# A hybrid attention / state-space / mixture-of-experts layer: queries and keys computed with channels on partitions instead of tokens

## The chip, the cores and the metric

The kernel runs on one core of one Trainium2 chip. The metric is the device time of one execution in microseconds (us).

## The reference, cut to what matters

The layer normalises 1024 latent tokens and 256 context tokens, multiplies them by one wide weight `w_in`, runs differential attention beside a bidirectional state-space scan, merges both, and then applies a mixture of experts. The change touches the part that makes queries and keys. Each of the 8 heads has two halves of 64 channels; latent tokens get a rotary embedding that pairs channel i with channel i + 32 of the half, context keys get none.

```
q, k, v, z, xbc, dt_raw, gates = jnp.split(h @ w_in, IN_SPLITS, axis=-1)
q = apply_rope(q.reshape(nb, ns, N_ATTN_HEADS, 2, ATTN_DH), cos, sin)
k = apply_rope(k.reshape(nb, ns, N_ATTN_HEADS, 2, ATTN_DH), cos, sin)
kc = (hc @ w_k).reshape(nb, nl, N_ATTN_HEADS, 2, ATTN_DH)
k_all = jnp.concatenate([kc, k], axis=1)
s = jnp.einsum('bqhcd,bkhcd->bchqk', q, k_all) * ATTN_SCALE
```

```
def apply_rope(u, cos, sin):
    rot = jnp.concatenate([-u[..., 32:], u[..., :32]], axis=-1)
    return u * cos[:, None, None, :] + rot * sin[:, None, None, :]
```

## The kernel before, in words

Products in float32 accuracy are made of three matmuls on split operands: high by high, low by high and high by low (`mm3`; hi, lo are the two parts of the weights, hh, hl those of the normalised tokens). The order of all instructions is set when the kernel is built, by a planner (the class of `F`): every job is a generator that says what it needs next, and the planner advances the job that its own cost clocks find ready first. The engines then run their parts of that order one instruction after the other.

`norm_and_qkv` is the first stage. It computes six blocks of 512 columns of `w_in`, in the order k0, v0, q0, k1, v1, q1; a block holds four heads. `weights()` loads a block in two halves (`raw`) and splits them, the cast to `hi` on ACT and the subtraction to `lo` on DVE. `main()` in `norm_and_qkv` then takes the tiles of 128 tokens one after the other (two of context and eight latent ones for k and v, eight for q). For every tile the tokens are the stationary operand (128x128) and the 512 weight columns move: 24 matmuls into one of four PSUM banks (`acc`). So tokens stand on partitions in the result. Scores need channels on partitions, so `post_qk` does this for each tile of q or k: three rope operations on DVE (`ra`, and `rb` twice), an addition on POOL (`r`), four transposes on PE (`tr<-cst,r`), a cast of the transposed tile on ACT (`sa`) and the subtraction of the low part on DVE (`sb`). After every second tile SP issues the stores of `sa` and `sb` to the DRAM tensors `qk[0]` and `qk[1]`. These hold [128, 3328] for a half of a head in one piece: 64 channels by high and by low part, and in a row the queries twice and the keys.

Beside that, `ada_late` runs chains of multiply-adds on DVE (`wacc<-wada,cc,wacc`, chunks of eight instructions) and small matmuls on PE (`adab`). Before the first tiles PE also transposes the tokens (`tr<-cst,x`), and DVE and ACT normalise and split them.

The next stage begins with the dt job, whose matmuls `acc<-hh,hi 64x512` are the first after q1: it ends in a chain that goes from PE (`aux<-fold`) over DVE, ACT (absolute value, exponential, logarithm) and DVE back to PE (`aux<-dtn`). The matmuls of the convolution's inputs (`acc<-hh,hi 128x512`) follow.

Much later `attention_ahead` loads a half of a head at a time into a ring of three SBUF tiles `qk` ([128, 3328], 1664 KB). POOL issues these loads (`F.swdma`, line 1338); a load is issued when PE has finished with the tile whose place it takes. PE's scores `sps<-qk` wait for it.

The rotary table `rope` is loaded once, as [128, 8, 128] (512 KB).

Of the kernel before, what the change touches and what calls it, by code (L numbers as in the profile page):

```python
# [9 lines left out]
F32 = mybir.dt.float32  # L10
# [39 lines left out]
def host_consts():  # L50
    j = np.arange(P)
    eye = np.eye(P, dtype=np.float32)
    le = (j[:, None] <= j[None, :]).astype(np.float32)
    ge = (j[:, None] >= j[None, :]).astype(np.float32)
    ones = np.ones((P, P), np.float32)
    cst = np.concatenate([eye, le, ge, ones], axis=1)
    row = np.repeat(np.arange(T // 64, dtype=np.float32), 64)
    col = np.tile(np.arange(64, dtype=np.float32), T // 64)
    inv = np.float32(10000.0) ** (-np.arange(0, 32, 2, dtype=np.float32) / np.float32(32))
    inv = inv.astype(np.float32)  # L60
    ang = np.concatenate([row[:, None] * inv, col[:, None] * inv], axis=-1)
    cos, sin = np.cos(ang), np.sin(ang)
    rope = np.concatenate([cos, cos, -sin, sin], axis=-1).astype(np.float32)
    e = np.arange(64)
    iota = np.zeros((P, 260 + sum(LEVELS)), np.float32)
    iota[:, 0:64] = e
    iota[:64, 64:128] = e[None, :] < e[:, None]
    iota[:, 128:192] = np.tile((e[:8, None] > e[None, :8]).reshape(-1), 1)
    iota[:, 192], iota[:, 193], iota[:, 194] = j, j // 64, j // 32
    iota[:, 196:260] = CAPS  # L70
    slots = [j % (P // ways(min(P, c - P * lv))) + P * lv for lv, nr in enumerate(LEVELS) for c in CAPS[:nr]]
    iota[:, 260:] = np.stack(slots, axis=1)
    return {"cst": cst, "rope": rope, "iota": iota}
# [303 lines left out]
class Layer:  # L377
# [114 lines left out]
    def norm_and_qkv(s):  # L492
# [25 lines left out]
        cw = ap.tile([P, KC, 32], F32, name="cw")  # L518
        F.dma(craw[:, 0, :], I["c"].rearrange("b (p k) -> p (b k)", p=P))
        F.dma(craw[:, 1, :], I["c_ctx"].rearrange("(p k) -> p k", p=P))  # L520
        st = {"wa": [], "x": 0, "w": 0, "normed": 0, "mod": 0, "done": [set(), set(), set()], "cols": 0, "blocks": 0, "ada": False, "q": None, "two": {}}
        AX0, AW0, QS, NH = (2, 2, 4, 4, 6, 6, 8, 8, 8, 8), (2, 6), (0, 2, 1, 3), 3
        blocks = [("k", 0), ("v", 0), ("q", 0), ("k", 1), ("v", 1), ("q", 1)]
        ready = []
# [103 lines left out]
        def parts(g, k, hf, w):  # L628
# [5 lines left out]
            hfs.put(hf)  # L634
            st["done"][g].add(k)

        def weights():
            for n, (kind, j) in enumerate(blocks):
                c0 = {"q": COL_Q, "k": COL_K, "v": COL_V}[kind] + j * 512
                for a in (0, 4):  # L640
                    yield [raws, lambda: st["x"] >= (10 if n else AW0[a // 4]), "NOW"]
                    raw = raws.get()
                    F.dma(raw, win[:, a:a + 4, c0:c0 + 512])
                    st["w"] += 1
                    yield [lambda: sets[n % 2] is not None]
                    his, los = sets[n % 2]
                    yield [raw, his, los, "ACT"]
                    hi, lo = his.get(), los.get()
                    yield from s.splits([(hi[:, b:b + 2], lo[:, b:b + 2], raw[:, b:b + 2]) for b in (0, 2)],
                                        lambda raw=raw, w=(hi, lo): (raws.put(raw), ready.append(w)), 1)  # L650

        def post_v(ps, j, tok):
# [6 lines left out]
            F.dma(s.vv[j][tok], v[:, :512].rearrange("p (h d) -> p h d", d=P))  # L659
            sas.put(v)  # L660

        def post_qk(ps, kind, j, t):
            yield [lambda: st["q"] is not None]
            rr, ras, rbs, sas, sbs, rope = (st["q"][n] for n in ("r", "ra", "rb", "sa", "sb", "rope"))
            if t < 2:
                yield [ps, rr, "ACT"]
                r = rr.get()
                F.acopy(r, ps.rearrange("p (h x) -> p h x", x=64))
                acc.put(ps)
            else:  # L670
                yield [ps, rope, ras, rbs, "DVE"]
                cs = rope[:, t - 2, :]
                pv = ps.rearrange("p (h x) -> p h x", x=64)
                ra, rb = ras.get(), rbs.get()
                F.tt(ra, pv, cs[:, None, 0:64].to_broadcast([P, 8, 64]), ALU.mult)
                F.tt(rb[:, :, 0:32], pv[:, :, 32:64], cs[:, None, 64:96].to_broadcast([P, 8, 32]), ALU.mult)
                F.tt(rb[:, :, 32:64], pv[:, :, 0:32], cs[:, None, 96:128].to_broadcast([P, 8, 32]), ALU.mult)
                acc.put(ps)
                yield [ra, rb, rr, "POOL"]
                r = rr.get()  # L680
                F.ptt(r, ra, rb, ALU.add)
                ras.put(ra)
                rbs.put(rb)
            yield [r, tr]
            pt = tr.get()
            for m in range(4):
                F.tp(pt[:, m * P:(m + 1) * P], r[:, 2 * m:2 * m + 2].rearrange("p u x -> p (u x)"), s.ident)
            two = st["two"].setdefault((kind, j, t // 2), [])
            yield [pt, "ACT"] + ([] if two else [sas, sbs])
            if not two:  # L690
                two += [sas.get(), sbs.get(), 0]
            a, b = two[:2]
            (av, bv), pv = (w.rearrange("p (m h c) -> h p m c", m=4, h=2)[t % 2] for w in (a, b)), pt.rearrange("p (m c) -> p m c", m=4)
            F.acopy(av, pv)
            yield [a, "DVE"]
            F.tt(bv, pv, av.bitcast(F32), ALU.subtract)
            tr.put(pt)
            two[2] += 1
            if two[2] == 2:
                o0 = (t // 2 - (kind == "q")) * 2 * P  # L700
                dst = s.qk[j].rearrange("(m u) (v x) c -> v u x m c", u=2, v=2)
                for w, v, o in ((a, 0, 0), (a, 1, 0), (b, 0, T), (b, 1, T)) if kind == "q" else ((a, 0, 2 * T), (b, 1, 2 * T)):
                    for u in range(2):
                        F.dma(dst[v, u][:, :, o + o0:o + o0 + 2 * P], w[64 * u:64 * u + 64].bitcast(F32).rearrange("x (m c) -> x m c", m=4))
                sas.put(a)
                sbs.put(b)
            rr.put(r)

        def main():
            for n, (kind, j) in enumerate(blocks):  # L710
                tiles = list(range(2 if kind == "q" else 0, 10))
                steps = [(t, 0, KC) for t in tiles]
                if n == 0:
                    steps = [(t, a, a + 4) for a in (0, 4) for t in tiles[:NH]] + steps[NH:]
                banks = {}
                for t, k0, k1 in steps:
                    yield [lambda: len(ready) >= 2 * n + k1 // 4]
                    tok = slice(t * P, (t + 1) * P)
                    g = 0 if t < 2 else 1 if t < 6 else 2
                    sl = slice((t - spans[g][0]) * P, (t - spans[g][0] + 1) * P)  # L720
                    hh, hl = s.h[g]
                    yield [lambda: st["done"][g].issuperset(range(k0, k1))] + ([] if k0 else [acc])
                    ps = banks.pop(t) if k0 else acc.get()
                    for k in range(k0, k1):
                        wh, wl = ready[2 * n + k // 4]
                        if k % 4 == 0:
                            yield [wh, wl, hh, hl]
                        s.mm3(ps, hh[:, k, sl], hl[:, k, sl], wh[:, k % 4], wl[:, k % 4], k == 0, k == KC - 1)
                    if k1 < KC:
                        banks[t] = ps  # L730
                    else:
                        F.spawn(1, post_v(ps, j, tok) if kind == "v" else post_qk(ps, kind, j, t))
                ws = ready[2 * n:2 * n + 2]
                his, los = sets[n % 2]
                for hi, lo in ws:
                    his.put(hi)
                    los.put(lo)
                st["blocks"] = n + 1
# [8 lines left out]
        F.run(lambda: st["ada"])  # L747
        s.close("wa")
        qp = s.open("qkv", side="right")
        st["q"] = q = {"r": s.ring(qp, [P, 8, 64], "r", 2), "ra": s.ring(qp, [P, 8, 64], "ra", 2),  # L750
                       "rb": s.ring(qp, [P, 8, 64], "rb", 2), "sa": s.ring(qp, [P, 1024], "sa", 2, F32R),
                       "sb": s.ring(qp, [P, 1024], "sb", 2, F32R), "rope": qp.tile([P, 8, P], F32, name="rope")}
        F.dma(q["rope"], I["rope"].rearrange("(t p) c -> p t c", p=P))
        F.run(lambda: len(st["done"][2]) == KC)
        s.close("xp")
        qw = s.open("qkvw1", side="right")
# [569 lines left out]
    def attention_ahead(s, go):  # L1326
# [5 lines left out]
        def loads():  # L1332
            yield [go]
            for h in range(8):
                for c in range(2):
                    yield [s.qks, "POOL"]
                    t = s.qks.get()
                    F.swdma(t, s.qk[h // 4][2 * (h % 4) + c])
                    s.heads[h, c] = t

        F.spawn(2, s.lam(qp))
# [1159 lines left out]
```

## Time and profile before

| what | value |
| --- | --- |
| times of three runs | 2753.43, 2750.43, 2750.11 us (median 2750.43) |
| the profiled execution | 2762.38 us, of which its span is 2760.1 us |
| mean granted TensorE clock of the span | 0.979 of full speed |
| TensorE (PE) busy | 2610.2 us, 95% of the span |
| VectorE (DVE), ScalarE (ACT), GpSimd (POOL) busy | 73%, 49%, 33% of the span |
| chain that ended last | PE 63%, DMA 8%, DVE 8% of the span |
| the six blocks of q, k, v on PE | from 31.9 to 387.7 us of the span |

The profiled execution took 11.95 us (0.43%) more than the median of the three runs. In the rows, times are microseconds and the mean of one instruction is in nanoseconds; L149 is the line of the helper that issues every matmul, L153 that of every transpose, so instructions are told apart by the tiles they write and read (`out<-in`). PEclk is the granted clock of TensorE as a part of full speed (2.4 GHz).

### The profile page before, as it was taken

The page shows a single profiled execution, that of the slowest core. Times are in us where ns is not written, and L with a number is a line of the kernel's source. Part 1 is how long each engine was busy: PE and PEld are TensorE (multiplying, and loading weights), DVE is VectorE, ACT ScalarE, POOL GpSimd, SP SyncE. Part 2 cuts the span into 40 slices and gives each one's busy share as a digit, 9 for nine tenths or more (in the row PEclk, how much of TensorE's full clock was granted, in tenths as well). Part 3 has the DMA queues.
Part 4 walks back from the last instruction along what each step waited for, and adds up shares of the span by engine and source line. Part 5 has one row for each costly group of instructions (what it writes and reads, how often), then busy time and mean ns, then how long its engine had stood idle before and what let it go on. Part 6 is the DMA issues. An engine that isn't in the chain of part 4 may idle for free.

```text
span 2760.1 us, 41127 instructions
## 1 busy us (share of the span) xinstructions
PE 2610.2 (95%) x14561; PEld 2099.0 (76%) x14561; DVE 2012.4 (73%) x4680; ACT 1341.9 (49%) x2104; POOL 920.9 (33%) x669
## 2 busy tenths in 40 slices
PE   7999999999999998999999999899999999999992
PEld 4888878878787776888888778677787787777771
DVE  6878133777776657888896657877879898888864
ACT  4211113344444446666675432335566666666652
POOL 0111010445354531000000000044667766777761
PEclk9999999999999999999999999999999999999996
DMA  7767253242425345322422872468999999999998
GB/s 275 226 205 220 62 149 102 69 145 77 138 77 149 91 120 186 119 86 87 142 97 75 263 252 107 168 234 288 292 319 315 339 333 311 315 314 307 296 308 251
DMA packets 275409, 545.67 MB, mean 198 GB/s; under 512 B 31562, under 2 KB 166835, under 8 KB 248194
## 3 DMA queue, kind: packets, MB, share of 16 engines
q1 hardware_dynamic: 238178, 432.95, 46.0%
q0 software_dynamic: 35872, 105.88, 14.7%
q10 hardware_dynamic: 1152, 4.19, 0.4%
q8 instruction: 115, 1.88, 0.3%
q14 instruction: 92, 0.75, 0.1%
HBM read 433.78 MB, written 124.73 MB: 202 GB/s over the span
## 4 chain that ended last, share of the span: by engine, by line
PE 63%; DMA 8%; DVE 8%; issue 3%; POOL 2%; ACT 2%; SPq 0%; ACTq 0%; POOLq 0%; DVEq 0%
PE gu L149 18%; PE acc L149 11%; PE dn L149 9%; PE bacc L149 6%; PE sps L149 5%; PE pv L149 4%; PE xt L153 3%; DMA cr<-cumd,crow 2%; PE tr L153 2%; PE aux L149 2%; DVE G L188 2%; DMA qk<-qk 2%; PE py L149 1%; DVE W L181 1%; PE hT L153 1%
## 5 line engine op out<-in xcount | busy, mean ns | idle before, releaser
L149 PE MATMUL acc<-hh,hi 128*128 128x512 f32 (+2 forms) x760 | 304.8, 401 | 1.3 <-DVE ux L188 1.3
L172 DVE TENSOR_TENSOR gl<-raw,gh 128x1024 fp32r<-128x1024 f32 x240 | 288.7, 1218 | 19.7 <-ACT gh L165 19.4
L149 PE MATMUL acc<-hl,hi 128*128 128x512 f32 (+2 forms) x760 | 289.5, 381 | 0.0
L149 PE MATMUL acc<-hh,lo 128*128 128x512 f32 (+1 forms) x736 | 281.0, 382 | 3.0 <-DVE lo L172 3.0
L149 PE MATMUL gu<-gh,xh 128*128 128x512 f32 (+3 forms) x672 | 279.5, 416 | 0.0
L149 PE MATMUL gu<-gh,xl 128*128 128x512 f32 (+3 forms) x672 | 264.6, 394 | 0.0
L149 PE MATMUL gu<-gl,xh 128*128 128x512 f32 (+3 forms) x672 | 264.3, 393 | 0.2 <-DVE gl L172 0.2
L165 ACT CAST gh<-raw 128x1024 fp32r<-128x1024 f32 x240 | 246.0, 1052 | 30.6 <-PE gu L149 21.2
L263 POOL DMA_INDIRECT cr<-cumd,crow x98 | 134.1, 1368 | 319.0 <-DMA wtab<-sc 282.5
L194 DVE TENSOR_SCALAR_CACHE_REDUCE e<-sps 128x512 f32<-128x512 f32 (+1 forms) x384 | 214.4, 597 | 33.9 <-PE sps L149 33.6
L269 POOL DMA_INDIRECT yacc<-y,tk x98 | 189.4, 1933 | 80.8 <-DMA yacc<-y,tk 14.4
L149 PE MATMUL sps<-qk 128*128 128x512 f32 (+1 forms) x768 | 196.1, 387 | 11.2 <-DMA qk<-qk 6.1
L157 ACT ACTIVATE e<-e,st 128x1280 f32<-128x1280 f32 x128 | 174.8, 1366 | 31.8 <-DVE st L203 31.6
L263 POOL DMA_INDIRECT wc<-wtab,tk x98 | 153.8, 1570 | 86.5 <-DVE tk L183 58.3
L149 PE MATMUL acc<-hi,hh 128*128 128x512 f32 x448 | 182.0, 406 | 0.0
L149 PE MATMUL acc<-hi,hl 128*128 128x512 f32 x448 | 176.6, 394 | 0.4 <-DVE hl L172 0.4
L149 PE MATMUL acc<-lo,hh 128*128 128x512 f32 x448 | 176.6, 394 | 0.0
L149 PEld LDWEIGHTS sps<-qk 128*128 128x128 f32 x768 | 141.4, 192 | 43.9 <-DVE e L194 9.8
L149 PEld LDWEIGHTS acc<-hh,hi 128*128 128x128 f32 (+1 forms) x760 | 142.5, 187 | 32.7 <-issue 4.2
L149 PE MATMUL pv<-wr,vv 128*128 128x256 f32 x640 | 164.6, 380 | 0.0
L149 PEld LDWEIGHTS acc<-hh,lo 128*128 128x128 f32 x736 | 138.8, 189 | 32.9 <-DVE lo L172 4.0
L149 PEld LDWEIGHTS acc<-hl,hi 128*128 128x128 f32 (+1 forms) x760 | 142.6, 188 | 27.4 <-issue 0.8
(327 smaller groups left out, 6246.5 us busy)
## 6 DMA issues: line engine op xcount, KB each, us to landing
raw<-in_w_e_gate_dram SPq DMA_DIRECT2D x64, 1024.0 KB, 9.2
raw<-in_w_e_up_dram SPq DMA_DIRECT2D x64, 1024.0 KB, 11.4
draw<-in_w_e_down_dram SPq DMA_DIRECT2D x64, 1024.0 KB, 9.9
qk<-qk POOLq DMA_DIRECT2D x16, 1664.0 KB, 10.4
raw<-in_w_in_dram SPq DMA_DIRECT2D x40, 512.0 KB, 4.7
wada<-in_w_ada_dram SPq DMA_DIRECT2D x32, 512.0 KB, 5.6
R<-acd SPq DMA_DIRECT2D x64, 256.0 KB, 5.4
qk<-sa SPq DMA_DIRECT2D x52, 256.0 KB, 4.1
```

The lines of the kernel that those rows point to most:

```text
L149: s.nc.tensor.matmul(out, l, r, start=start, stop=stop)
L153: s.nc.tensor.transpose(out, in_, ident)
L157: s.nc.scalar.activation(out, in_, fn, **kw)
L165: s.nc.scalar.copy(out, in_)
L172: s.nc.vector.tensor_tensor(out, a, b, op=op)
L181: s.nc.vector.tensor_scalar(out, a, s1, s2, op0=op0)
L188: s.nc.vector.scalar_tensor_tensor(out, a, sc, b, op0=op0, op1=op1)
L194: s.nc.vector.tensor_scalar(out, a, s1, None, op0=op0, op1=op1, accum_out=acc)
L263: s.nc.gpsimd.indirect_dma_start(out=out, out_offset=None, in_=table, in_offset=bass.IndirectOffsetOnAxis(ap=idx, axis=0), **kw)
L269: s.nc.gpsimd.indirect_dma_start(out=table, out_offset=bass.IndirectOffsetOnAxis(ap=idx, axis=0), in_=in_, in_offset=None, compute_op=ALU. ...
```

## The change

Queries and keys are computed with the weights as the stationary operand. `weights()` writes the split weights of q and k in another order (`byhalf`): first the 32-channel halves that rope pairs (f = 0, 1), then the eight 128-row pieces. A unit of work of `main()` in `norm_and_qkv` is (g, r, f): a group of tokens g (0 the 256 context tokens, 1 and 2 each 512 latent ones), a half r of the block's heads and a rope half f. 128 channels stand still and 256 or 512 tokens move. The result has channels on partitions, and the two units f = 0, 1 are the partners of the rotation, so `post_qk` takes a pair of banks: four products of 128x512 on DVE, a subtraction and an addition on POOL, two casts on ACT and two subtractions on DVE; context pairs are only cast and subtracted, 256 wide. There are no transposes. Each block of k now has 24 stores instead of 20 and each block of q still 32 (112 in all instead of 104), each from 128 partitions with one piece of 1 or 2 KB per partition, still issued by SP. `qk` is filled as plain blocks of 128 rows, and a load of a head's half now reads 32 rows from each of four blocks. The rotary table becomes [128, 2, 1024] (1 MB). The tiles `r` and `ra` go, `rb` is [128, 2, 512].

```diff
-    rope = np.concatenate([cos, cos, -sin, sin], axis=-1).astype(np.float32)
+    rope = np.stack([np.tile(q.T, (4, 1)) for q in (cos, sin)], axis=1).astype(np.float32)
...
+        def byhalf(w):
+            return w.rearrange("p a b -> p (a b)").rearrange("p (f k c) -> p f k c", f=2, k=4)
...
-        def post_qk(ps, kind, j, t):
+        def post_qk(pair, kind, j, g, r):
...
-                F.tt(ra, pv, cs[:, None, 0:64].to_broadcast([P, 8, 64]), ALU.mult)
-                F.tt(rb[:, :, 0:32], pv[:, :, 32:64], cs[:, None, 64:96].to_broadcast([P, 8, 32]), ALU.mult)
-                F.tt(rb[:, :, 32:64], pv[:, :, 0:32], cs[:, None, 96:128].to_broadcast([P, 8, 32]), ALU.mult)
...
-                F.ptt(r, ra, rb, ALU.add)
...
-            for m in range(4):
-                F.tp(pt[:, m * P:(m + 1) * P], r[:, 2 * m:2 * m + 2].rearrange("p u x -> p (u x)"), s.ident)
...
+                F.tt(l[0], pair[0], cos, ALU.mult)
+                F.tt(rb[:, 1], pair[0], sin, ALU.mult)
+                acc.put(pair[0])
+                yield [pair[1], "DVE"]
+                F.tt(rb[:, 0], pair[1], sin, ALU.mult)
+                F.tt(l[1], pair[1], cos, ALU.mult)
+                acc.put(pair[1])
+                yield [rb, "POOL"]
+                F.ptt(l[0], l[0], rb[:, 0], ALU.subtract)
+                yield [rb, "POOL"]
+                F.ptt(l[1], l[1], rb[:, 1], ALU.add)
...
+            for f in range(2):
+                yield [src[f], "ACT"]
+                F.acopy(hi[:, f * 512:f * 512 + n], src[f])
+            for f in range(2):
+                yield [hi, "DVE"]
+                F.tt(l[f], src[f], hi[:, f * 512:f * 512 + n].bitcast(F32), ALU.subtract)
...
+            dst = s.qk[j].rearrange("(r v f) p c -> r v f p c", v=2, f=2)
...
+                    units = [(g, r, f) for g in ((0, 1, 2) if kind == "k" else (1, 2)) for r in range(2) for f in range(2)]
+                    if n == 0:
+                        units = units[4:6] + units[:4] + units[6:]
...
+                            a, b = (byhalf(w)[:, u[2], k % 4, u[1] * P:(u[1] + 1) * P] for w in (wh, wl))
+                            s.mm3(ps[:, :spans[g][1] * P], a, b, hh[:, k], hl[:, k], k == 0, k == KC - 1)
...
-                    F.swdma(t, s.qk[h // 4][2 * (h % 4) + c])
+                    F.swdma(t, s.qk[h // 4].rearrange("(r x) (y i) c -> r y x i c", x=4, y=4)[h % 4 // 2, h % 2 * 2 + c])
```

The planner sees other costs and needs, so the order of the first stage moves. Three places, all on PE. The first is the start: `acc<-wa,cw` and `adab<-fold,row` make the modulation vector, `hh_81` and `hl_82` are the context tokens, `hh_83` and `hl_84` the first 512 latent ones, `hi_172` is the first half of k0's weights. Before:

```order
L149 MATMUL acc<-wa,cw 32x512 x4
L149 MATMUL acc<-hi_172,hh_81 128x512
L149 MATMUL acc<-lo_173,hh_81 128x512
L149 MATMUL acc<-hi_172,hl_82 128x512
...
L149 MATMUL adab<-fold,row 128x2 x4
L153 MATMUL tr<-cst,x_89 128x128
```

And with the change:

```order
L149 MATMUL acc<-wa,cw 32x512 x8
L149 MATMUL adab<-fold,row 128x2 x4
L153 MATMUL tr<-cst,x_89 128x128
...
L153 MATMUL tr<-cst,x_88 128x128
L149 MATMUL acc<-hh_83,hi_172 128x512
L149 MATMUL acc<-hl_84,hi_172 128x512
L149 MATMUL acc<-hh_83,lo_173 128x512
```

Before, 24 matmuls of the first two tiles stand ahead of the latent tokens' transposes; now the first matmul of k0 stands behind 20 of these transposes and behind the rest of the modulation.

The second place is the end of q1, where the dt job follows (`acc<-hh_83,hi 64x512`). Before:

```order
L149 MATMUL acc<-hi_2477,hh_85 128x512
L149 MATMUL acc<-lo_2478,hh_85 128x512
L149 MATMUL acc<-hi_2477,hl_86 128x512
L153 MATMUL tr<-cst,r 128x128 x8
L149 MATMUL acc<-hh_83,hi 64x512
```

And with the change:

```order
L149 MATMUL acc<-hh_85,hi_2366 128x512
L149 MATMUL acc<-hl_86,hi_2366 128x512
L149 MATMUL acc<-hh_85,lo_2367 128x512
L149 MATMUL acc<-hh_83,hi 64x512
L149 MATMUL acc<-hl_84,hi 64x512
```

The eight transposes of the last two tiles are gone, and dt follows q1 at once.

The third place is the end of the dt job, where the convolution's matmuls begin (`acc<-hh_83,hi 128x512`). Before:

```order
L149 MATMUL aux<-fold,G 128x32 x10
L149 MATMUL acc<-hh_83,hi 128x512
L149 MATMUL acc<-hl_84,hi 128x512
L149 MATMUL acc<-hh_83,lo 128x512
...
L149 MATMUL aux<-dtn,cst 128x160
```

And with the change:

```order
L149 MATMUL aux<-fold,G 128x32 x10
L149 MATMUL aux<-dtn,cst 128x160 x2
L149 MATMUL aux<-dtn,cst 128x320
L149 MATMUL aux<-cst,dtn 16x128 x4
L149 MATMUL acc<-hh_83,hi 128x512
```

Nine of the convolution's matmuls stood between `aux<-fold` and the first `aux<-dtn`; now none does. From the convolution on, the order of every engine is the same in both kernels, but for the form of the 16 loads of `qk`.

## Rows read from the trace of the kernel before

**Rows 1.** the page, part 1: busy us, share of the span and instructions of the engines

```profile
PE 2610.2 (95%) x14561; PEld 2099.0 (76%) x14561; DVE 2012.4 (73%) x4680; ACT 1341.9 (49%) x2104; POOL 920.9 (33%) x669
```

**Rows 2.** busy time by stretch: us, PE, PEld, DVE, ACT, POOL, clock, DMA, GB/s

```profile
40.00:80.00 40.00, 37.20 (x214) 29.04 (x214) 36.26 (x88) 22.89 (x36) 2.64 (x2) 1.00 0.49 159
120.00:200.00 80.00, 79.96 (x371) 65.48 (x371) 59.55 (x150) 12.11 (x18) 5.98 (x4) 1.00 0.71 218
```

**Rows 3.** instructions by line and form, 0 to 400 us: count | busy, mean ns | idle before, releaser

```profile
L188 DVE SCALAR_TENSOR_TENSOR wacc<-wada,cc,wacc 128x128 f32<-128x128 f32 x224 | 88.1, 393 | 8.0
...
L153 PE MATMUL tr<-cst,r 128*128 128x128 f32 x144 | 22.2, 276 | 5.7 <-POOL r L176 5.6
...
L172 DVE TENSOR_TENSOR ra<-acc,rope 128x512 f32<-128x512 f32 x32 | 22.0, 688 | 28.1 <-PE acc L149 26.3 <-PE adab L153 1.7
...
L165 ACT CAST sa<-tr 128x512 fp32r<-128x512 f32 x36 | 21.1, 586 | 147.1 <-PE tr L153 133.8 <-issue 13.2
```

**Rows 4.** timeline of PE around one group of transposes: start, us, instruction, [idle <-releaser]

```profile
84.45 0.39 PE L149 MATMUL acc<-hi,hl 128*128 128x512 f32 x1
84.68 0.60 PE L153 MATMUL tr<-cst,r 128*128 128x128 f32 x4
85.03 0.48 PE L149 MATMUL acc<-hi,hh 128*128 128x512 f32 x1
85.35 0.40 PE L149 MATMUL acc<-lo,hh 128*128 128x512 f32 x1
```

**Rows 5.** timeline of PE in q1, at one of its first groups of transposes

```profile
347.16 0.40 PE L149 MATMUL acc<-hi,hl 128*128 128x512 f32 x1
...
349.86 0.71 PE L153 MATMUL tr<-cst,r 128*128 128x128 f32 x4 [2.30 <-POOL r L176]
...
350.27 0.73 PE L149 MATMUL acc<-hi,hh 128*128 128x512 f32 x1
...
353.77 0.40 PE L149 MATMUL acc<-hi,hl 128*128 128x512 f32 x1
```

**Rows 6.** timeline of PE at the end of q1 and the start of dt

```profile
387.65 0.60 PE L153 MATMUL tr<-cst,r 128*128 128x128 f32 x4
...
390.76 0.66 PE L153 MATMUL tr<-cst,r 128*128 128x128 f32 x4 [2.51 <-POOL r L176]
...
391.17 0.67 PE L149 MATMUL acc<-hh,hi 128*64 128x512 f32 x1
...
394.63 0.43 PE L149 MATMUL acc<-hh,hi 128*64 128x512 f32 x1
```

**Rows 7.** timeline of PE in a later stage, matmuls of 256 columns

```profile
663.09 0.28 PE L149 MATMUL acc<-hh,hi 128*128 128x256 f32 x1
...
663.44 0.28 PE L149 MATMUL acc<-hh,hi 128*128 128x256 f32 x1
```

**Rows 8.** timeline of PE at the start, first and last early matmul of k0

```profile
31.94 0.80 PE L149 MATMUL acc<-hi,hh 128*128 128x512 f32 x1
...
38.93 0.40 PE L149 MATMUL acc<-hi,hl 128*128 128x512 f32 x1
```

**Rows 9.** timeline of PE at the end of the dt job

```profile
404.54 0.50 PE L149 MATMUL acc<-hh,hi 128*128 128x512 f32 x1
...
409.10 0.54 PE L149 MATMUL aux<-dtn,cst 128*128 128x160 f32 x2 [0.25 <-DVE dtn L188]
```

**Rows 10.** the chain of waits in attention: start, us, what

```profile
1095.95 7.68 DMA qk<-qk
```

**Rows 11.** who waited for whom, PE, 1040 to 1500 us: us, times, longest

```profile
PE sps L149 <- DMA qk<-qk: 6.1, 6, 3.3
```

**Rows 12.** busy time by stretch, columns as in rows 2, first attention loads and first boundary

```profile
1049.00:1056.00 7.00, 7.00 (x32) 5.82 (x31) 0.22 (x1) 0.77 (x1) 0.00 (x0) 1.00 1.03 405
1095.90:1103.70 7.80, 6.84 (x39) 5.71 (x37) 7.34 (x25) 6.21 (x10) 2.12 (x3) 1.00 0.85 286
```

More of the change, by code (lines that the diff above doesn't have):

```diff
@@ L520, in norm_and_qkv @@
         F.dma(craw[:, 1, :], I["c_ctx"].rearrange("(p k) -> p k", p=P))
-        st = {"wa": [], "x": 0, "w": 0, "normed": 0, "mod": 0, "done": [set(), set(), set()], "cols": 0, "blocks": 0, "ada": False, "q": None, "two": {}}
+        st = {"wa": [], "x": 0, "w": 0, "normed": 0, "mod": 0, "done": [set(), set(), set()], "cols": 0, "blocks": 0, "ada": False, "q": None}
         AX0, AW0, QS, NH = (2, 2, 4, 4, 6, 6, 8, 8, 8, 8), (2, 6), (0, 2, 1, 3), 3
@@ L648, in weights @@
                     hi, lo = his.get(), los.get()
-                    yield from s.splits([(hi[:, b:b + 2], lo[:, b:b + 2], raw[:, b:b + 2]) for b in (0, 2)],
+                    parts = [[w[:, b:b + 2] for w in (hi, lo, raw)] for b in (0, 2)]
+                    if kind != "v":
+                        parts = [[byhalf(w)[:, :, b:b + 2].rearrange("p f k (y i) -> p f (k y) i", i=32) for w in (hi, lo)] +
+                                 [raw[:, b:b + 2].rearrange("p k (y f i) -> p f (k y) i", f=2, i=32)] for b in (0, 2)]
+                    yield from s.splits(parts,
                                         lambda raw=raw, w=(hi, lo): (raws.put(raw), ready.append(w)), 1)
@@ L660, in post_v @@
             sas.put(v)
-        def post_qk(ps, kind, j, t):
+        def post_qk(pair, kind, j, g, r):
             yield [lambda: st["q"] is not None]
[L664 to L674, printed above, removed]
-                F.tt(ra, pv, cs[:, None, 0:64].to_broadcast([P, 8, 64]), ALU.mult)
-                F.tt(rb[:, :, 0:32], pv[:, :, 32:64], cs[:, None, 64:96].to_broadcast([P, 8, 32]), ALU.mult)
-                F.tt(rb[:, :, 32:64], pv[:, :, 0:32], cs[:, None, 96:128].to_broadcast([P, 8, 32]), ALU.mult)
-                acc.put(ps)
-                yield [ra, rb, rr, "POOL"]
-                r = rr.get()
-                F.ptt(r, ra, rb, ALU.add)
-                ras.put(ra)
-                rbs.put(rb)
-            yield [r, tr]
-            pt = tr.get()
-            for m in range(4):
-                F.tp(pt[:, m * P:(m + 1) * P], r[:, 2 * m:2 * m + 2].rearrange("p u x -> p (u x)"), s.ident)
[L688 to L707, printed above, removed]
@@ new lines, in post_qk @@
+            rbs, sas, sbs, rope = (st["q"][n] for n in ("rb", "sa", "sb", "rope"))
+            n = spans[g][1] * P
+            yield [sbs, pair[0]]
+            lo = sbs.get(F32)
+            l = [lo[:, f * 512:f * 512 + n] for f in range(2)]
+            if g:
+                cos, sin = (rope[:, i, (g - 1) * 512:g * 512] for i in range(2))
+                yield [pair[0], rope, rbs, "DVE"]
+                rb = rbs.get()
+                F.tt(l[0], pair[0], cos, ALU.mult)
[9 more added lines that the diff above has]
+                F.ptt(l[1], l[1], rb[:, 1], ALU.add)
+                rbs.put(rb)
@@ new lines, in post_qk @@
+            src = l if g else [b[:, :n] for b in pair]
+            yield [sas]
+            hi = sas.get()
+            for f in range(2):
[4 more added lines that the diff above has]
+                F.tt(l[f], src[f], hi[:, f * 512:f * 512 + n].bitcast(F32), ALU.subtract)
+            if g == 0:
+                acc.put(*pair)
+            o0 = (spans[g][0] - 2 * (kind == "q")) * P
@@ L709, in main @@
+            dst = s.qk[j].rearrange("(r v f) p c -> r v f p c", v=2, f=2)
+            for f in range(2):
+                for w, v, o in ((hi, 0, 0), (hi, 1, 0), (lo, 0, T), (lo, 1, T)) if kind == "q" else ((hi, 0, 2 * T), (lo, 1, 2 * T)):
+                    F.dma(dst[r, v, f][:, o + o0:o + o0 + n], (w[:, f * 512:f * 512 + n].bitcast(F32) if w is hi else l[f]))
+            sas.put(hi)
+            sbs.put(lo)
         def main():
             for n, (kind, j) in enumerate(blocks):
-                tiles = list(range(2 if kind == "q" else 0, 10))
@@ L712, in main @@
-                steps = [(t, 0, KC) for t in tiles]
+                if kind == "v":
+                    units = [(0 if t < 2 else 1 if t < 6 else 2, t) for t in range(10)]
+                else:
+                    units = [(g, r, f) for g in ((0, 1, 2) if kind == "k" else (1, 2)) for r in range(2) for f in range(2)]
+                    if n == 0:
+                        units = units[4:6] + units[:4] + units[6:]
+                steps = [(u, 0, KC) for u in units]
                 if n == 0:
-                    steps = [(t, a, a + 4) for a in (0, 4) for t in tiles[:NH]] + steps[NH:]
@@ L715, in main @@
-                banks = {}
-                for t, k0, k1 in steps:
+                    steps = [(u, a, a + 4) for a in (0, 4) for u in units[:NH]] + steps[NH:]
+                banks, done = {}, {}
+                for u, k0, k1 in steps:
+                    g = u[0]
                     yield [lambda: len(ready) >= 2 * n + k1 // 4]
-                    tok = slice(t * P, (t + 1) * P)
-                    g = 0 if t < 2 else 1 if t < 6 else 2
-                    sl = slice((t - spans[g][0]) * P, (t - spans[g][0] + 1) * P)
@@ L721, in main @@
                     hh, hl = s.h[g]
                     yield [lambda: st["done"][g].issuperset(range(k0, k1))] + ([] if k0 else [acc])
-                    ps = banks.pop(t) if k0 else acc.get()
+                    ps = banks.pop(u) if k0 else acc.get()
                     for k in range(k0, k1):
@@ L727, in main @@
                             yield [wh, wl, hh, hl]
-                        s.mm3(ps, hh[:, k, sl], hl[:, k, sl], wh[:, k % 4], wl[:, k % 4], k == 0, k == KC - 1)
+                        if kind == "v":
+                            sl = slice((u[1] - spans[g][0]) * P, (u[1] - spans[g][0] + 1) * P)
+                            s.mm3(ps, hh[:, k, sl], hl[:, k, sl], wh[:, k % 4], wl[:, k % 4], k == 0, k == KC - 1)
+                        else:
+                            a, b = (byhalf(w)[:, u[2], k % 4, u[1] * P:(u[1] + 1) * P] for w in (wh, wl))
+                            s.mm3(ps[:, :spans[g][1] * P], a, b, hh[:, k], hl[:, k], k == 0, k == KC - 1)
                     if k1 < KC:
-                        banks[t] = ps
-                    else:
-                        F.spawn(1, post_v(ps, j, tok) if kind == "v" else post_qk(ps, kind, j, t))
+                        banks[u] = ps
+                    elif kind == "v":
+                        F.spawn(1, post_v(ps, j, slice(u[1] * P, (u[1] + 1) * P)))
+                    else:
+                        two = done.setdefault(u[:2], [])
+                        two.append(ps)
+                        if len(two) == 2:
+                            F.spawn(1, post_qk(two, kind, j, *u[:2]))
                 ws = ready[2 * n:2 * n + 2]
@@ L749, in norm_and_qkv @@
         qp = s.open("qkv", side="right")
[L750 to L753, printed above, removed]
+        st["q"] = q = {"rb": s.ring(qp, [P, 2, 512], "rb", 2),
+                       "sa": s.ring(qp, [P, 1024], "sa", 2, F32R),
+                       "sb": s.ring(qp, [P, 1024], "sb", 2, F32R), "rope": qp.tile([P, 2, T], F32, name="rope")}
+        F.dma(q["rope"], I["rope"])
         F.run(lambda: len(st["done"][2]) == KC)
```

## The prediction

> **What bounds the kernel now.** I read the page first: PE is busy for 2610.2 of 2760.1 us [rows 1], so time is won only where PE does less or waits less. Next I read busy time by stretch inside the stage that changes. From 40 to 80 us DVE works 36.26 of 40 us and PE 37.20, so the start is shared between them; from 120 to 200 us PE works 79.96 of 80 us and DVE 59.55 [rows 2], so from there on PE alone sets the pace and DVE, ACT and POOL lie beside it. Then the groups of instructions by line: the 144 transposes of q and k (36 groups of four) are PE work that the change takes out [rows 3]. Last the timeline of PE, which shows what a group costs between matmuls and where PE stood idle for one. Behind the first stage the order of every engine is unchanged, so what the stage gains or loses carries through to the end. The exception is the 16 attention loads, which keep their place and change their form.
>
> **The sum for the first stage.** The profiled execution took 2762.38 us.
>
> Transposes. From 84.45 to 85.35 us two matmuls and one group went by in 0.90 us [rows 4]; two matmuls at the 0.23 us of the first two rows are 0.46, so a group costs 0.44. Nine groups lie in k0, before 110.7 us, and are counted with the start. The other 27 give 27 x 0.44 = **-11.9 us**.
>
> Two idle stretches. In q1 the transposes waited 2.30 us for POOL's addition `r` [rows 5]: from 347.16 to 350.27 is 3.11 us for work worth 0.23 + 0.44, so 2.4 is lost. After it the clock was down: eight matmuls took from 350.27 to 353.77, 3.50 us, where 8 x 0.233 = 1.87 is normal, so another 1.6. The last group waited 2.51 us, and again eight matmuls took 3.46 us [rows 6]. The change leaves no PE instruction behind a POOL addition in this stage, so both go: 2.4 + 1.6 + 2.5 + 1.6 = **-8.1 us**. What is late next is the bank: a unit needs a free `acc`, which DVE's products release.
>
> Narrow matmuls. Three matmuls of 256 columns went by in 0.35 us [rows 7], 0.117 each. In k1 192 of them replace 96 of 512: 192 x 0.117 - 96 x 0.233 = **+0.1 us**.
>
> The start. Before, 24 matmuls ran between 31.94 and 38.93 us [rows 8], when PE otherwise waited for tokens and modulation. With the change none do, so 24 x 0.233 = 5.6 us of work moves to a time when PE is short. The nine groups that go from k0 give back 4.0. PE also comes to its first long run of matmuls after waits, and one run-up at the low clock costs the 1.6 of rows 5. Walking through the new order of PE and DVE with the durations of before, I get k0's end 2.1 us later, narrow matmuls included; with the run-up I take **+3.6 us**. The bounds are 0 (DVE, at 36.26 of 40 us, hides the moved work) and +8 (the groups' gain is lost as well).
>
> From q0 to k1. Two chains of eight `wacc` instructions (393 ns each in [rows 3]; 8 x 0.39 = 3.1 us) now stand on DVE between the two halves of a pair's rope, in front of a bank that k1's fourth unit needs. k1 begins with four short units of 24 x 0.117 = 2.8 us: three of them, 8.4 us, cover 2 x 3.1 us of chains and four products at 688 ns [rows 3], 9.0 us in all. That is nearly balanced; I take **+2.5 us**, with bounds of 0 (the chains ran ahead) and +5 (they start when the last unit ends).
>
> From dt to the convolution. The chain from the last `aux<-fold` to the first `aux<-dtn` took from 404.54 to 409.10 us, 4.56 us, in which PE did nine matmuls, worth 2.1 [rows 9]. Now nothing stands between, so PE idles for all of it: +2.1. The convolution's first weights are also cast behind the logarithm on ACT, and PE falls to the low clock (+1.6, as in rows 5). I take **+4 us**, with bounds of +2 and +6.
>
> At nothing. For 512 tokens by 512 columns the elements stay the same: DVE had four `ra` and eight half-wide `rb`, now eight products, and four subtractions in both; POOL has four operations of 512 in both, ACT four casts (586 ns, [rows 3]). What could cost is their views, runs of 32 in the weights' split above all; DVE has 20 of 80 us free and ACT 68 [rows 2], and that hides it. Without that cover, a tenth more on DVE would be 6 us per 80. The eight more stores and the larger rope table go through SP, and no PE instruction waits for them.
>
> Sum: -11.9 - 8.1 + 0.1 + 3.6 + 2.5 + 4.0 = **-9.8 us**, 2752.6 for the profiled execution. That execution lies 11.95 us above the median of the runs, so against the median the forecast is **2740.6 us**. All low bounds together (0, 0, +2) give -17.9, all high ones (+8, +5, +6) give -0.9: this case has 2732 to 2750.
>
> **The attention loads.** Each of the eight heads but the first begins with a load of 1664 KB that PE needs at once. The first boundary's load stands in the chain of waits with 7.68 us [rows 10], and PE waited for such loads six times, 6.1 us in all, up to 3.3 us [rows 11]: the other work at a boundary hides nearly 7 us and nothing more. So every microsecond that this load gets longer is one on PE's path, seven times. The new load moves the same bytes in the same rows of 13 KB, to the same 128 partitions, but its source is four blocks of 32 rows and no longer 128 rows in one piece. The forecast takes it as equal, since rows, length and destination are the same. No row of before shows a load from POOL whose source has four outer pieces, so that is the weakest step.
>
> **Rival 1, slower: the load runs on a part of the DMA engines.** If a transfer is dealt out by the outer pieces of its source, four of the 16 engines carry it. In the stretch in which the engines were most loaded, 16 of them moved 405 GB/s at a share of 1.03 [rows 12], 25.3 GB/s each. At the first boundary they moved 286 GB/s at 0.85, 21 GB/s each. 1664 KB are 1.70 MB, so four engines need 16.8 to 20.3 us. The fixed part is the 7.68 us of rows 10 less the 5.5 us that the 2.23 MB of that stretch (286 x 7.8) take at 405 GB/s, 2.2 us. The load takes 19 to 22.5 us in place of 7.7: +11.3 to +14.8. I take +12, and the low clock after each wait, +1.6: 7 x 13.6 = +95 us, which makes **2836 us** (2790 if half of it is hidden, 2875 at the high bounds with the first head late too). It decides as soon as a load needs more than 2 us longer: 7 x 2 is more than the sum above. For it speaks that the source's form is all that changed in this load; against it, that the 128 partitions of the destination can be dealt out as before, and the rows are long. I give it 0.41.
>
> The Trainium skill, page "DMA: Bandwidth & Descriptors", section "Why a DMA increments its semaphore by 16 and not by 1", says that a DMA gets the largest number of engines, up to 16, that divides the slowest dimension of both its sides. By that rule a source of four blocks and a destination of 128 partitions would get four engines and rival 1 would hold; the rule names an exception in which some direct copies from the queue of these loads still get 16, and then the forecast would hold. No run here shows which of the two it is.
>
> **Rival 2, no change: the start and the bank waits give it all back.** If DVE, whose stretch from 40 to 80 us is 91% full, sets the end of k0 and its rope work stands in the way of PE's banks in q0 and q1, the three upper bounds hold, +19 us, against the 20.0 that go: -0.9, some **2749.5 us**. For it: a pair holds two of the four banks until its products are done, 4 x 688 ns, and chains of `wacc` stand between them. Against it: from 120 us on DVE has a quarter of its time free [rows 2]. I give it 0.12.
>
> **How the numbers follow.** The forecast has 0.47, rival 1 0.41, rival 2 0.12. A measurement of this kernel can tell about 0.2%, 5.5 us, from no change. Of the forecast's 0.47, 0.43 lie over 5.5 us below the median and 0.04 within it; rival 2 has 0.02 faster, 0.07 within and 0.03 slower; rival 1 is all slower. So faster 0.45, same 0.11, slower 0.44. Cases of both signs hold most of the chance: the likeliest one's own range is 2732 to 2750 us. The range that should hold 8 times in 10 reaches from 2733 into rival 1, over its value, to 2860.
>
> **What would show it.** In the profile afterwards: no `tr<-cst,r`; PE at 0.227 to 0.233 us per matmul of 512 columns through q0 and q1, with no wait for POOL; the first matmul of dt some 12 us earlier than the 391.17 of rows 6 (27 groups, both idle stretches and one slow run-up gone, 11.9 + 2.4 + 1.6 + 2.5, less 6.2 for the start, k1's matmuls and its wait); then an idle PE of some 4.5 us before `aux<-dtn`; and the attention loads landing in 7 to 10 us with PE waits of about 1 us. Landings near 20 us at the head boundaries, with PE idle for over 10 us each time, would make rival 1 right and the forecast wrong by about 95 us. PE waits on DVE for `acc` in every pair of q would make rival 2 right.

## The result, and the profile after

The changed kernel takes 3007.97 us (median of four runs) against 2751.93 for the kernel before: a ratio of 1.0925, 95% interval 1.0908 to 1.0942, 256 us slower. The forecast said 2740.6 us, faster; its range ended at 2860. Rival 1 had the right place and direction, but not the size.

The page of the changed kernel, busy time of the engines, answers to [rows 1]. PE's busy time is the same 2610.2 us (some matmuls fewer, others at a lower clock), but the span around it is 3013.2 us instead of 2760.1:

```profile
PE 2610.2 (87%) x14513; PEld 2102.8 (70%) x14513; DVE 2013.1 (67%) x4652; ACT 1342.2 (45%) x2104; POOL 925.9 (31%) x669
```

Who waited for whom, PE, whole span (us in total, times, longest us), answers to [rows 11], where the same wait was 6.1 us in six times:

```profile
PE sps L149 <- DMA qk<-qk: 261.7, 8, 68.9
```

The list of DMA issues (size, median us from issue to landing) has the reason. The line of before ended in 10.4:

```profile
qk<-qk POOLq DMA_DIRECT2D x16, 1664.0 KB, 37.2
```

The timeline of PE shows eight waits, one before the first head (68.87 us, the first wait below) and one at each of the seven boundaries between heads (23.10 to 28.67 us). Three of them stand here:

```profile
1107.05 3.31 PE L149 MATMUL sps<-qk 128*128 128x512 f32 x8 [68.87 <-DMA qk<-qk]
...
1184.51 2.47 PE L149 MATMUL sps<-qk 128*128 128x512 f32 x6 [28.67 <-DMA qk<-qk]
...
1681.57 2.47 PE L149 MATMUL sps<-qk 128*128 128x512 f32 x6 [23.10 <-DMA qk<-qk]
```

Busy time by stretch (columns as in [rows 2]; clock, DMA share and GB/s last) shows the second wait and what follows. Nothing works, the clock is at its lower level (0.50), 108 to 114 GB/s arrive, and then PE works 6 us at a mean clock of 0.61:

```profile
1160.00:1170.00 10.00, 0.00 (x0) 0.00 (x0) 0.00 (x0) 0.00 (x0) 0.00 (x0) 0.50 0.56 114
1170.00:1180.00 10.00, 0.00 (x0) 0.00 (x0) 0.00 (x0) 0.00 (x0) 0.00 (x0) 0.50 0.52 108
...
1184.00:1190.00 6.00, 5.49 (x21) 4.76 (x22) 2.50 (x8) 1.23 (x3) 0.00 (x0) 0.61 0.49 96
```

The first stage did win. POOL's timeline shows when the first three attention loads are issued, before and with the change: 15.5 us earlier.

```profile
1041.50 1.82 POOL L228 DMA_DIRECT2D qk<-qk  x3
```

```profile
1025.96 2.26 POOL L228 DMA_DIRECT2D qk<-qk  x3
```

So the account is: waits for loads +255.6 us (261.7 - 6.1); the low clock after each wait +15 (from the first score matmuls behind a wait to the next group took 4.88 us after 1184.51 and 2.98 at the same boundary before, 1.9, measured at this boundary and taken for all eight waits, so an estimate); first stage -15.5. Together +255, where the spans differ by 253.1.

### The profile page after: what moved, and what is told of

The parts are those of the page before. It is cut to its first block, busy times and chain, and to the rows that moved or that the text cites. A ratio compares the mean times of both kernels' runs of the same rounds, so it can differ in the third digit from the quotient of the medians.

```text
span 3013.2 us, 41008 instructions
## 1 busy us (share of the span) xinstructions
PE 2610.2 (87%) x14513; PEld 2102.8 (70%) x14513; DVE 2013.1 (67%) x4652; ACT 1342.2 (45%) x2104; POOL 925.9 (31%) x669
## 5 line engine op out<-in xcount | busy, mean ns | idle before, releaser
L149 PE MATMUL sps<-qk 128*128 128x512 f32 (+1 forms) x768 | 203.8, 399 | 266.8 <-DMA qk<-qk 261.7
L149 PE MATMUL acc<-hh,hi 128*128 128x512 f32 (+3 forms) x1080 | 425.6, 394 | 1.3 <-DVE ux L188 1.3
L149 PE MATMUL acc<-hl,hi 128*128 128x512 f32 (+3 forms) x1080 | 408.0, 378 | 0.0
L149 PE MATMUL acc<-hh,lo 128*128 128x512 f32 (+1 forms) x1056 | 400.2, 379 | 2.4 <-DVE lo L172 2.4
L165 ACT COPY wr<-tr 128x512 f32<-128x512 f32 x160 | 93.4, 584 | 317.2 <-PE tr L153 316.7
L149 PEld LDWEIGHTS acc<-hh,hi 128*128 128x128 f32 (+1 forms) x1080 | 203.1, 188 | 43.1 <-issue 2.7
L149 PEld LDWEIGHTS acc<-hh,lo 128*128 128x128 f32 x1056 | 199.7, 189 | 42.9 <-DVE lo L172 2.9
L149 PEld LDWEIGHTS acc<-hl,hi 128*128 128x128 f32 (+1 forms) x1080 | 203.3, 188 | 37.2
L269 POOL DMA_INDIRECT yacc<-y,tk x98 | 187.8, 1916 | 81.7 <-DVE y L181 12.2
L228 POOL DMA_DIRECT2D qk<-qk x16 | 11.0, 690 | 512.0 <-PE sps L149 512.0
L263 POOL DMA_INDIRECT xg<-htab,tk x98 | 131.9, 1346 | 85.1 <-PE hT L153 52.3
```

The lines of the kernel that those rows point to most:

```text
L149: s.nc.tensor.matmul(out, l, r, start=start, stop=stop)
L165: s.nc.scalar.copy(out, in_)
L228: s.nc.gpsimd.dma_start(out, in_)
L263: s.nc.gpsimd.indirect_dma_start(out=out, out_offset=None, in_=table, in_offset=bass.IndirectOffsetOnAxis(ap=idx, axis=0), **kw)
L269: s.nc.gpsimd.indirect_dma_start(out=table, out_offset=bass.IndirectOffsetOnAxis(ap=idx, axis=0), in_=in_, in_offset=None, compute_op=ALU. ...
```

## The experiments

Theory A: a load is carried by as many DMA engines as its source has outer pieces. Theory B: four separate regions of DRAM, or the way that rows are cut into packets, make it slow on whatever engines. Theory C: it is what the new first stage left in DRAM or left running. Times are compared with the kernel before in the same set of runs (2751.9 us for the first four, 2770.0 for the next two, 2763.1 for the last; they ran on different chips).

### The load alone, and the compute alone

The first run puts the new load into the kernel before, the second puts the old load into the changed kernel:

```diff
-                    F.swdma(t, s.qk[h // 4][2 * (h % 4) + c])
+                    F.swdma(t, s.qk[h // 4].rearrange("(r x) (y i) c -> r y x i c", x=4, y=4)[h % 4 // 2, h % 2 * 2 + c])
```

```diff
-                    F.swdma(t, s.qk[h // 4].rearrange("(r x) (y i) c -> r y x i c", x=4, y=4)[h % 4 // 2, h % 2 * 2 + c])
+                    F.swdma(t, s.qk[h // 4][2 * (h % 4) + c])
```

> The kernel before with nothing changed but the attention load, which takes 32 rows from each of four blocks as the change does; since the old compute fills the tensor differently, the scores are made from other rows, and the work is the same. Theory A (a load is carried by as many DMA engines as its source has outer pieces, four): the 16 loads land in about 37 us as in the changed kernel, PE waits some 260 us for them, and the time is that of before plus about 265 us, 3010 to 3030. Theory B (four separate regions in DRAM, or rows cut into other packets, make the load slow on whatever engines): the same. Theory C (the load is slow because of how the new stores laid the data in DRAM, or because of what the new first stage leaves running): loads land in 7 to 10 us and the time is that of before.

> The changed kernel with the attention load of before (128 rows in one piece); the scores are made from other rows than the reference's, and the work is the same. Theories A and B: the loads land in 7 to 10 us again, PE waits for them 5 to 8 us in all, and what is left is the first stage: 11 to 17 us faster than before, 2735 to 2741. Theory C: the loads stay at about 37 us and the time near 3000.

The load alone gave 3052.7 us, above the 3010 to 3030 expected, and much the same waits of PE as the changed kernel (261.7 us in eight), here from 1000 us on:

```profile
PE sps L149 <- DMA qk<-qk: 253.0, 8, 62.1
```

Theory C falls: the old first stage with the new load is as slow. With the old load in the changed kernel the waits are gone (1000 to 1500 us):

```profile
PE sps L149 <- DMA qk<-qk: 3.0, 6, 0.9
```

The first stage's gain stayed (the first loads are issued at 1025.56), but the total was 2768.0 us, ratio 1.0060 (1.0038 to 1.0082), and not the 2735 to 2741 expected. The reading is that the other rows in the scores sent tokens to other experts: PE waits for a gather for which it waits neither before nor in the changed kernel, and does 46 matmuls and transposes more (14559 against 14513). The wait alone is a good half of the excess:

```profile
PE bank L153 <- DMA oxg<-htab,otk: 17.2, 1, 17.2
```

The first run has this wait too, with 17.4 us. So these two totals say nothing to within 1%; the waits in attention do.

### Pieces: four DMAs, eight pieces, two pieces

```diff
-                    F.swdma(t, s.qk[h // 4].rearrange("(r x) (y i) c -> r y x i c", x=4, y=4)[h % 4 // 2, h % 2 * 2 + c])
+                    for x in range(4):
+                        F.swdma(t[32 * x:32 * x + 32], s.qk[h // 4].rearrange("(r x) (y i) c -> r y x i c", x=4, y=4)[h % 4 // 2, h % 2 * 2 + c][x])
```

> The changed kernel, with each load of a head's half issued as four DMAs of 32 rows, each with one piece as its source; same regions, same rows. Theory A: each of the four has 32 rows to deal out and gets all 16 engines, so the half is there after 8 to 12 us; POOL issues four times as often (4 x 0.55 us); the time is 2736 to 2750, faster than before or equal. Theory B: four regions stay four regions, the half lands after 30 us or more, and the time is near 3000.

It took 2769.9 us, ratio 1.0073 (1.0054 to 1.0093): 238 us of the 256 are back, with the same four regions, and theory B has no place left for its cost. But it is no gain. The halves land 9 to 11 us after their issue at a boundary. At the first head POOL issues eight DMAs, then waits for a landing before each further one, and PE waits 9.2 us for branch weights (`bwh`); from the first issue to the load for the first boundary it took 70.6 us (1024.88 to 1095.48), where the last run of this section took 53.4 (1025.36 to 1078.73). That is 17 of some 37 us between the two runs, each taken against its own before; where the rest went was not traced. The stretches around the first boundary show all 16 engines busy, at little more than half of the 405 GB/s of [rows 12]:

```profile
1100.00:1104.00 4.00, 2.29 (x14) 1.70 (x12) 3.72 (x11) 3.38 (x5) 0.79 (x2) 1.00 1.09 213
1104.00:1110.00 6.00, 3.78 (x13) 3.28 (x14) 3.24 (x10) 0.76 (x2) 0.00 (x0) 0.72 1.07 236
```

Eight pieces in one DMA:

```diff
+                    F.swdma(t, s.qk[h // 4].rearrange("a (y i) c -> y a i c", y=8)[2 * (h % 4) + c])
```

> The changed kernel, with a load that takes 16 rows from each of eight blocks, 128 rows and the same bytes; the scores are made from other rows than the reference's. Theory A: eight engines carry it, so the load lands in about half of 37.2 us, 17 to 21; a boundary waits some 11 us instead of 27, and the time is 2800 to 2870. Theory B: twice as many regions, so 37 us or more, and the time is 3000 or above.

2855.5 us; the loads land in 20.9 us, and the waits are well under half:

```profile
PE sps L149 <- DMA qk<-qk: 101.9, 8, 13.8
```

More regions, less time: theory A, within its numbers. Two pieces:

```diff
+                    F.swdma(t, s.qk[h // 4].rearrange("(r x) (y i) c -> r y x i c", x=2, y=2)[h % 4, c])
```

> The changed kernel with a load that takes 64 rows from each of two blocks; the scores are made from other rows than the reference's. Theory A (as many engines as outer pieces): two engines, at the 12 GB/s each that four and eight engines had, 1.70 MB in some 71 us; a boundary waits about 64 us and the first head longer, PE waits over 500 us in all and the time is above 3200. The packets tell it too: the queue of these loads had 2048 packets more than before with eight pieces (16 loads x 128 rows x 1) and 6144 more with four (16 x 128 x 3); by the same rule two pieces give 16 x 128 x 7 = 14336 more, some 50200. Theory B (each further region in DRAM costs): two regions are cheaper than four, landing under 37 us, time under 3000.

The time, 3023.3 us, met neither: two engines were expected to make it 3200, and two regions to make it cheaper than four. The chain of waits has the loads at 37 to 41 us, as with four pieces. The packets decide on the number of engines. The queue that carries these loads (packets, MB, share of 16 engines) in the kernel before, with four, eight and two pieces:

```profile
q0 software_dynamic: 35872, 105.88, 14.7%
```

```profile
q0 software_dynamic: 42016, 105.91, 17.2%
```

```profile
q0 software_dynamic: 37920, 105.89, 17.3%
```

```profile
q0 software_dynamic: 50208, 105.94, 14.1%
```

50208 is the number that was expected. The additional packets are as many as idle engines times the rows that each working engine carries: 16 loads x 12 x 32 = 6144 with four engines, 16 x 8 x 16 = 2048 with eight, 16 x 14 x 64 = 14336 with two. The busy share of the 16 engines agrees. While two loads were under way and nothing else, it was 0.52 to 0.56 with four pieces (above; two loads on four engines each are 0.50), and with two pieces it was 0.27, two loads on two engines each:

```profile
1136.00:1146.00 10.00, 0.00 (x0) 0.00 (x0) 0.00 (x0) 0.00 (x0) 0.00 (x0) 0.60 0.27 95
1146.00:1156.00 10.00, 0.00 (x0) 0.00 (x0) 0.00 (x0) 0.00 (x0) 0.00 (x0) 0.50 0.27 105
```

So theory A holds for the number of engines, as far as packets and share show it, and the rate of an engine is what the expectation had wrong. With two pieces an engine moves 105 / 4 = 26 GB/s, as in [rows 12]; with four it moves 114 / 8 = 14, and with eight 208 / 16 = 13 (in the row below all 16 are busy with two loads):

```profile
1112.00:1116.00 4.00, 0.00 (x0) 0.00 (x0) 0.00 (x0) 0.00 (x0) 0.00 (x0) 0.50 1.06 208
```

### Why four engines move no more than two

Two theories for the rate: R, it goes with the number of pieces in a DMA; S, two engines share one rate when they write certain blocks of partitions at the same time, 0 to 31 with 32 to 63, and 64 to 95 with 96 to 127.

```diff
-                    F.swdma(t, s.qk[h // 4].rearrange("(r x) (y i) c -> r y x i c", x=4, y=4)[h % 4 // 2, h % 2 * 2 + c])
+                    for x in (0, 2):
+                        F.swdma(t[32 * x:32 * x + 64], s.qk[h // 4].rearrange("(r x) (y i) c -> r y x i c", x=4, y=4)[h % 4 // 2, h % 2 * 2 + c][x:x + 2])
```

> The changed kernel, with each half of a head loaded by two DMAs of 64 partitions, each with two outer pieces of 32 rows; same data. With four pieces in one DMA the four engines moved 12 to 14 GB/s each, with two pieces in one DMA the two engines 25.6 each. Theory R (a DMA on fewer engines pays per engine by its own count of pieces: two pieces run at 25 GB/s each): 2 x 2 engines at 25 GB/s, landing 19 to 22 us, a boundary waits about 13 us, time about 110 us above before's. Theory S (two engines get half of their rate each when they write partitions 0 to 31 and 32 to 63, or 64 to 95 and 96 to 127, at the same time, whichever DMA they belong to; in the run with two pieces they wrote 0 to 63 and 64 to 127): 2 x 2 engines at 13 GB/s, landing 33 to 38 us, a boundary waits 25 to 30 us, time about 240 to 260 us above before's. In both, 14 idle engines per DMA get a small packet for each of 32 rows: 16 x 2 x 14 x 32 = 14336 more packets than before in the queue (and 512 to close the additional DMAs).

2983.4 us, 220 above before's 2763.1, a little less than S said. The chain of waits (start, us) has 34 to 37 us at all seven boundaries, of which the first three stand here, where R said 19 to 22:

```profile
1129.99 36.64 DMA qk<-qk
1215.59 35.97 DMA qk<-qk
1298.19 37.13 DMA qk<-qk
```

R falls, and S fits this pair of runs: two pieces over 128 partitions run at 26 GB/s an engine, two pieces over 64 do not. The pair does not show S, since it differs in the source too: two blocks of 64 rows against four blocks of 32, so what counts may also be which blocks are read at the same moment. The run below shows only that reading these four blocks is not slow in itself. The packets are 50464, the 14336 expected and 256 to close 16 additional DMAs; the 512 in the expectation counted twice as many.

### The same gather, rows first

```diff
-                    F.swdma(t, s.qk[h // 4].rearrange("(r x) (y i) c -> r y x i c", x=4, y=4)[h % 4 // 2, h % 2 * 2 + c])
+                    F.swdma(t, s.qk[h // 4].rearrange("(r x) (y i) c -> r y i x c", x=4, y=4)[h % 4 // 2, h % 2 * 2 + c])
```

> The changed kernel with the same gather from the same four blocks, only that the load's source runs over the 32 rows first and over the four blocks inside: the channels of a half stand in another order on the partitions, the same for queries and keys, so that the scores are the reference's. Theory A: 32 outer pieces, 16 engines; the loads land in 7 to 11 us, no extra packets (35872 in the queue), PE waits for them 5 to 8 us in all; the time is that of before less the first stage's gain, 2733 to 2741, and so the fastest of all. Theory B: four regions as before, 37 us, near 3000.

One letter changes its place: the 32 rows are the outer count of the source, the four blocks the inner. Scores sum over the partitions, so their order is free as long as queries and keys share it. It took 2750.9 us against 2770.0 of before on the same chip, ratio 0.9927 (0.9913 to 0.9942), so 20 us faster than before, the fastest version here. The queue's packets are those of before, two loads at once move 437 GB/s, and PE hardly waits (1000 to 1500 us):

```profile
q0 software_dynamic: 35872, 105.88, 14.9%
```

```profile
1139.50:1143.50 4.00, 4.00 (x25) 3.48 (x24) 3.93 (x13) 3.48 (x8) 0.00 (x0) 1.00 1.08 437
```

```profile
PE sps L149 <- DMA qk<-qk: 1.1, 2, 0.8
```

The 20 us are the 16 of the first stage and some 5 of waits for loads. The expected 2733 to 2741 was meant against 2752. As a part of before that is 0.993 to 0.996, and the measured 0.9927 lies at its lower end.

## Why the prediction was wrong, and where it was right

**The step that failed** is "The forecast takes it as equal, since rows, length and destination are the same." They are the same, and the load still went from 7.7 to 35.5 us at a boundary (1149.05 to 1184.51), since its source is dealt out by its outermost count. The prediction had called it the weakest step and gave it more weight than its rival all the same. The argument against rival 1, that the 128 partitions of the destination can be dealt out as before, was the mistake: the destination had 128 partitions in the changed kernel and in the runs with two, eight and 32 outer pieces, and the source's count decided.

**Rival 1's size.** Its mechanism was right (four engines: packets and share), its terms were not. Rival 1 stood at 2836 us and 3007.97 were measured. An engine was priced at 21 to 25.3 GB/s from [rows 12], and four moved 12 to 14 each; the boundary was priced at +12 and cost 22 to 28. The low clock was priced at 1.6 and cost 1.9. The first head, mentioned only for the upper bound, waited 68.9 us. With the measured terms the rival's sum is 255.6 + 15, and its upper bound, 2875, was 133 us too low.

The Trainium skill's rule in "DMA: Bandwidth & Descriptors", section "Why a DMA increments its semaphore by 16 and not by 1", which the prediction set beside this rival, agrees with all these runs: two, four and eight engines for slowest dimensions of two, four and eight, sixteen for 32. The exception that it names did not hold for this load. The same page, section "The descriptor swizzle", says that in a transfer to 128 partitions the partitions 0 to 3 and 32 to 35 belong to the same port of SBUF. That fits theory S: engines that walk 0 to 31 and 32 to 63 side by side would meet at each port. The rates agree (26 against 13 GB/s); which port an engine uses no run here shows, and theory S is argued, not shown.

**The first stage**, point by point, from the timeline of PE in the changed kernel:

```profile
45.92 0.48 PE L149 MATMUL acc<-hh,hi 128*128 128x512 f32 x1
...
112.35 0.48 PE L149 MATMUL acc<-hi,hh 128*128 128x512 f32 x1
...
374.05 0.40 PE L149 MATMUL acc<-hh,hi 128*64 128x512 f32 x1
...
390.32 2.76 PE L149 MATMUL aux<-dtn,cst 128*128 128x160 f32 x6 [4.47 <-DVE dtn L188]
...
394.82 0.80 PE L149 MATMUL acc<-hh,hi 128*128 128x512 f32 x1
```

- The start: PE's first matmul of k0 went from 31.94 to 45.92 us, and k0 ended at 112.35 instead of 110.7, +1.6 where +3.6 was taken (bounds 0 to 8).
- From q0 to k1: PE has no idle stretch of over 0.4 us between 59 and 386 us, so the wait is nothing where +2.5 was taken. The lower bound was right.
- Transposes and the two idle stretches: dt begins at 374.05 instead of 391.17, 17.1 us earlier, where 12.2 was predicted. The two terms above make 4.5 of the 4.9, which leaves 0.4 for the -11.9 and the -8.1 together; they were not measured one by one.
- From dt to the convolution: PE idles 4.47 us, where some 4.5 were predicted. Once the nine matmuls are made up, the convolution stands 13.5 us ahead of before. From 17.1 that is 3.6, and the slow run-up of dt (1.6, booked with the idle stretches) had gone in between, so the term is +5.2 where +4 was taken (bounds 2 to 6).
- The sum to there is -13.5 against -9.8, and the rest of the scan stage wins another 2 before the attention loads. DVE, ACT, POOL and the stores cost nothing that PE shows, as predicted; rival 2 falls with that.

What stays open: why the first three loads, issued at once, needed 82 us together (a first wait of 68.9 us). From 1055 to 1105 us the DMA share was 0.78 to 0.90 and 64 to 77 GB/s arrived: if three loads keep 12 engines busy, that is 5 to 6 GB/s for each, an estimate that leaves out the 640 KB load `vv` issued right behind them, and under half of what two loads at once gave them. With two pieces the first wait was 34.5 us, and from 1045 to 1065 us 122 to 129 GB/s arrived at a share of 0.40 to 0.46, so six engines moved 20 to 22 each. That engines meet at the same ports could explain the first figure, but there too three engines walk over each half of the partitions; no run tried it by itself. The rate of an engine with four and eight pieces is open in the same way.

## What to carry to other kernels

When a layout moves, read each DMA's access pattern as the instruction carries it: the outermost count of the source set how many of the 16 engines carried these loads, and four blocks of 32 rows can be written as 32 rows of four blocks at no cost if the order on the partitions is free. A load that something waits for at every step deserves this look before any saving elsewhere: here 256 us hung on the order of two letters, beside a saving of 16. And a trial that feeds other data may change the work of a layer that routes tokens, so read it by its waits and not by its total.

## What the runs showed of the hardware that was not expected

- A load on fewer engines had more packets, as many as idle engines x rows per working engine: 384 per load with four engines, 128 with eight, 896 with two. The last number was forecast from the other two.
- Two engines were about as fast as four (37 to 41 us against 34 to 36 at a boundary, for 1664 KB), since each of the four moved half as much (14 against 26 GB/s); why is not shown. And DMAs of 32 partitions each moved 213 to 236 GB/s with all 16 engines busy, where DMAs of 128 partitions moved 405 to 437.
